# Three edits to a hybrid GLA/FoX/memory layer: an earlier accumulating load for the gates' seventh product, the first gate's T1 built by loads, and mask adds held behind a split

## The chip, the cores and the metric

The kernel runs on one core of one Trainium2 chip. The metric is the device time of one execution in microseconds; lower is better. The engines are named as in the profile: PE (TensorE, matmuls and turns), PEld (its weight loads), DVE (VectorE), ACT (ScalarE), POOL (GpSimd) and SP (SyncE, which here only issues loads). A DMA is issued by a queue of SP, ACT or POOL.

## The reference

One layer on 512 frames of width 1024, all in float32. Three branches read the same normed input `u`; each ends in a projection to width 1024, is weighted by a sigmoid gate, and the sum goes through one more projection.

```python
u = rmsnorm(h, g_mix[l])
proj = u @ w_in[l]
(gq, gk, gv, gg, ga, fq, fk, fv, ff, mq, gates) = split_cols(proj, PROJ_SIZES)
...                                  # branch A: chunked gated linear attention (GLA)
o_fox = forgetting_attention(...)    # branch B: softmax(q k^T * scale + F_t - F_s, causal) v, 8 heads
...                                  # branch C: cross attention into 256 memory tokens
gt = jax.nn.sigmoid(gates.reshape(B, S, N_BRANCH, D))
merged = gt[:, :, 0] * y_gla + gt[:, :, 1] * y_fox + gt[:, :, 2] * y_mem
h = h + merged @ w_out[l]
u2 = rmsnorm(h, g_ffn[l])
h = h + jnp.square(jax.nn.relu(u2 @ w_ff1[l])) @ w_ff2[l]
return rmsnorm(h, g_final)
```

## The kernel before

**Number format.** Every float32 matmul is made of three: each operand is split into a high part (a cast by ACT to the matmul's rounded float32, `hi`) and a low part (the rest, a subtraction by DVE, `lo`), and `mm3` (L163 to L166) issues hi x hi, hi x lo and lo x hi. So each 512 KB tile of weights (128 x 1024) costs one load, one ACT cast and one DVE subtraction, and PE follows them.

**Stages.** In order: memory keys and values, FoX projections and attention, memory attention, GLA, the three gates, output projection, MLP in four quarters. PE's order is written out by hand. The order of the other engines is set by a scheduler that simulates times, except inside `in_order(...)` (L131), where DVE, ACT and SP, and POOL too if it is named, keep the order of the program text. `tc.issue_after(x)` puts an instruction behind `x`.

**FoX.** Heads go in pairs `j`. For each head, `fox_rows` loads a row of decays, spread over all partitions, into `nFb` (L631, issued by ACT). `fox_masks` (L638) adds the causal mask to it in place: two DVE adds a head (L643). `fox_scores` (L645) uses `nFb` in the pair's scores (L670). `fox_turn` (L677) turns one head's probabilities on PE in three banks and splits each into `PTh` (ACT, L217) and `PTl` (DVE, L218); `fox_values` (L691) multiplies them with the values (L697, L698) and sums two halves into `oT` (L706). The list `steps` (L746 to L751) sets the sequence: scores of pair j, rows of pair j+1, values, turn of the even head, its values, masks of pair j+1, turn of the odd head. Projections and GLA weights are woven in between as filling for PE. In `live` lie things that one step leaves for another; `low_parts` (L619) issues put-off low parts behind a given instruction.

**Gates.** Each gate is a matrix product of `u` (512 x 1024) with a 1024 x 1024 weight, done in 2 x 2 blocks by Strassen's scheme in Winograd's form: seven products of blocks (256 x 512 times 512 x 512) instead of eight, in the order `ORDER = (1, 2, 5, 3, 6, 7, 4)`. There are three gates g = 0 (FoX), 1 (memory), 2 (GLA). A round (g, n) is one product: 2 row blocks t of 12 matmuls each, 24 in all. The weights of products 1, 2 and 3 are the blocks "11", "21" and "22" themselves. Products 5, 6, 4 and 7 need sums of blocks, two 512 KB tiles (c = 0, 1) each:

```python
# sum_tile(g, c, 0): "11" -> +"12" (T1, product 5) -> +"22" (product 6) -> +"21" (product 4)
# sum_tile(g, c, 1): "12" -> +"22" (product 7)
```

`load_sum` (L1073) loads the first block on SP's queue. `plus` (L1076) adds another with an accumulating DMA on POOL's queue (L1077). In `low` (L1092) the next `plus` on `sum_tile(g, c, 0)` follows the low part of products 1, 5 and 6. For the first gate, T1 is made another way: `gate_ready` (L988) loads and splits the blocks "11" for product 1 ahead of the gates, inside GLA, and keeps the raw tiles; `first_sum` (L1191) adds "12" to them on DVE after product 1's first half. Until then the tiles of T1 hold the weights of product 2.

Within a round the text's order is: `loads`; matmuls of t = 0; up to two merges of finished gate parts (for g = 1 also an add on POOL, L1171); casts and low parts of the next round's weights (`high`, `low`); `after`; matmuls of t = 1; evacuations of t = 0 and t = 1 (`evac`, L1129), copies on ACT (L1138, L1145, L1150), adds on DVE (L1053), and a tanh on ACT (L1125). Products 1, 6, 7 and 4 share a pair of banks, so product 4 must wait for the evacuation of product 7. `plus(g, c, 1, "22")` stands in `after` of round (g, 5).

Raw tiles that are not sums come from a ring of three (tag `raw`); the tiles of the sums (`h_tile`, tags h0 to h3) lie where GLA's inputs were and can be loaded once those have been read.

## Time and profile before

| | us |
|---|---|
| Median of 3 runs | 818.01 (817.62 to 818.79) |
| The profiled execution | 818.88 |
| Its span in the profile | 817.1 |
| PE busy | 798.7 (98%) |
| DVE busy | 606.6 (74%) |
| ACT busy | 459.3 (56%) |
| POOL busy | 104.9 (13%) |

All times in what follows are microseconds from the start of the span. In a row of a timeline, the bracket says how long the engine had been idle before and what ended that; `x2` means that two instructions are merged into one row. A profile's line number (L1094) is a line of the kernel; helpers such as `vec` (L1053) and `mm3` stand for many places. A releaser is inferred: where it had long been done, it was another, often a DMA.

### The profile page before, as it was taken

The page shows a single profiled execution, that of the slowest core. Times are in us where ns is not written, and L with a number is a line of the kernel's source. Part 1 is how long each engine was busy: PE and PEld are TensorE (multiplying, and loading weights), DVE is VectorE, ACT ScalarE, POOL GpSimd, SP SyncE. Part 2 cuts the span into 40 slices and gives each one's busy share as a digit, 9 for nine tenths or more (in the row PEclk, how much of TensorE's full clock was granted, in tenths as well). Part 3 has the DMA queues.
Part 4 walks back from the last instruction along what each step waited for, and adds up shares of the span by engine and source line. Part 5 has one row for each costly group of instructions (what it writes and reads, how often), then busy time and mean ns, then how long its engine had stood idle before and what let it go on. Part 6 is the DMA issues. An engine that isn't in the chain of part 4 may idle for free.

```text
span 817.1 us, 11695 instructions
## 1 busy us (share of the span) xinstructions
PE 798.7 (98%) x4375; PEld 681.3 (83%) x4375; DVE 606.6 (74%) x945; ACT 459.3 (56%) x733; POOL 104.9 (13%) x135
## 2 busy tenths in 40 slices
PE   9999999999999999998999999999999999999996
PEld 7888877888888877776888889987998899889985
DVE  6878788465545788768565568879799779988896
ACT  7756665444543445544442447775667367647764
POOL 0001000220210112146210000011001100110011
PEclk9999999999999999998999999999999999999998
DMA  9344654999994229796969723898858865895643
GB/s 354 137 168 168 223 208 163 267 248 277 299 325 162 93 105 221 220 178 175 219 149 251 263 79 115 273 234 214 248 180 183 219 217 181 188 274 201 162 84 123
DMA packets 40489, 164.39 MB, mean 201 GB/s; under 512 B 4848, under 2 KB 5552, under 8 KB 38064
## 3 DMA queue, kind: packets, MB, share of 16 engines
q0 software_dynamic: 10784, 61.87, 34.9%
q1 hardware_dynamic: 28288, 97.81, 33.3%
q10 hardware_dynamic: 1360, 3.96, 1.3%
q8 instruction: 34, 0.56, 0.3%
q14 instruction: 23, 0.19, 0.1%
HBM read 161.50 MB, written 35.68 MB: 241 GB/s over the span
## 4 chain that ended last, share of the span: by engine, by line
PE 75%; DMA 9%; DVE 6%; issue 5%; ACT 3%; POOL 1%; POOLq 0%; DVEq 0%; ACTq 0%
PE mm L1325 14%; PE mm L164 12%; PE mm L165 12%; PE mm L166 12%; PE a L164 4%; PE a L166 4%; PE a L165 4%; DMA wb<-in_wst_dram 4%; PE mm L1654 3%; DMA raw<-in_wst_dram 3%; PE mm L385 1%; DMA b<-in_wst_dram 1%; PE mm L1655 1%; PE a L398 1%; DVE wlo L155 1%
## 5 line engine op out<-in xcount | busy, mean ns | idle before, releaser
L1384 ACT CAST hi<-raw 128x1024 fp32r<-128x1024 f32 x52 | 54.5, 1048 | 37.4 <-PE mm L1325 19.2
L1385 DVE TENSOR_TENSOR lo<-raw,hi 128x1024 fp32r<-128x1024 f32 x52 | 63.6, 1223 | 13.5 <-ACT hi L1384 13.3
L155 DVE TENSOR_TENSOR wlo<-raw,whi 128x1024 fp32r<-128x1024 f32 x38 | 46.5, 1222 | 34.9 <-ACT whi L154 34.9
L1325 PE MATMUL mm<-u,hi 128*128 128x256 f32 x384 | 65.1, 283 | 0.0
L154 ACT CAST whi<-raw 128x1024 fp32r<-128x1024 f32 x38 | 39.9, 1050 | 44.2 <-PE mm L165 14.3
L1704 POOL DMA_DIRECT2D b<-in_wst_dram x30 | 25.7, 857 | 263.4 <-DVE lo L1385 130.4
L164 PE MATMUL mm<-uhl,whi 128*128 128x512 f32 x144 | 57.6, 400 | 0.0
L1325 PEld LDWEIGHTS mm<-u,hi 128*128 128x128 f32 x384 | 56.8, 191 | 0.3
L166 PE MATMUL mm<-uhl,wlo 128*128 128x512 f32 x144 | 56.3, 391 | 0.0
L165 PE MATMUL mm<-uhl,whi 128*128 128x512 f32 x144 | 56.2, 390 | 0.0
L165 PE MATMUL mm<-lo,ch 128*128 128x512 f32 (+1 forms) x132 | 51.2, 388 | 0.3 <-DVE lo L1385 0.3
L164 PE MATMUL mm<-hi,ch 128*128 128x512 f32 (+1 forms) x132 | 50.9, 386 | 0.0
L166 PE MATMUL mm<-hi,cl 128*128 128x512 f32 (+1 forms) x132 | 50.9, 386 | 0.0
L1325 PE MATMUL mm<-u2s,hi 128*128 128x256 f32 x288 | 47.6, 283 | 0.0
L1325 PE MATMUL mm<-u,lo 128*128 128x256 f32 x192 | 47.5, 283 | 0.0
L1384 ACT CAST hi<-b 128x1024 fp32r<-128x1024 f32 x26 | 27.3, 1048 | 29.3 <-PE mm L166 19.1
L1094 DVE TENSOR_TENSOR lo<-wb,hi 128x1024 fp32r<-128x1024 f32 x22 | 29.6, 1370 | 17.4 <-ACT hi L1090 17.4
L1325 PEld LDWEIGHTS mm<-u2s,hi 128*128 128x128 f32 x288 | 41.8, 192 | 0.3
L1385 DVE TENSOR_TENSOR lo<-b,hi 128x1024 fp32r<-128x1024 f32 x26 | 31.7, 1221 | 10.8 <-ACT hi L1384 10.8
L165 PE MATMUL a<-lo,ch 128*128 128x512 f32 (+1 forms) x96 | 37.1, 386 | 0.4 <-DVE lo L1442 0.4
L164 PE MATMUL a<-hi,ch 128*128 128x512 f32 (+1 forms) x96 | 37.0, 385 | 0.0
L166 PE MATMUL a<-hi,cl 128*128 128x512 f32 (+1 forms) x96 | 37.0, 385 | 0.0
(508 smaller groups left out, 2316.6 us busy)
## 6 DMA issues: line engine op xcount, KB each, us to landing
raw<-in_wst_dram SPq DMA_DIRECT2D x108, 512.0 KB
raw<-T SPq DMA_DIRECT2D x32, 512.0 KB
b<-in_wst_dram POOLq DMA_DIRECT2D x32, 512.0 KB, 5.2
T<-in_wst_dram POOLq DMA_DIRECT2D x12, 1024.0 KB, 18.2
wb<-in_wst_dram POOLq DMA_DIRECT2D x22, 512.0 KB, 8.0
b<-in_wst_dram SPq DMA_DIRECT2D x16, 512.0 KB
T<-in_wst_dram POOLq DMA_DIRECT2D x12, 512.0 KB, 7.4
wb<-in_wst_dram SPq DMA_DIRECT2D x12, 512.0 KB
```

Of the source, the lines that this page charges most:

```text
L154: cast = nc.scalar.copy(hi, raw)
L155: low_now[0] = nc.vector.tensor_tensor(lo, raw, f(hi), op=ALU.subtract).ins
L164: nc.tensor.matmul(ps, lh, rh, start=start, stop=False, skip_group_check=on)
L165: nc.tensor.matmul(ps, lh, rl, start=False, stop=False, skip_group_check=on)
L166: nc.tensor.matmul(ps, ll, rh, start=False, stop=stop, skip_group_check=on)
L385: nc.tensor.matmul(kps[h], w[:, h * P:(h + 1) * P], x[:, k, :], start=k == p == 0, stop=k == KT - 1 and p == 2)
L1094: nc.vector.tensor_tensor(lo, source(r, c), f(hi), op=ALU.subtract)
L1325: nc.tensor.matmul(ps[:, a, :], x[:, a, k, :], y[:, s, k, :], start=start, stop=stop, skip_group_check=go is not None)
L1384: split_now[0] = nc.scalar.copy(hi, raw).ins
L1385: split_now[1] = nc.vector.tensor_tensor(lo, raw, f(hi), op=ALU.subtract).ins
L1654: nc.tensor.matmul(ps, wh[:, a, k, :], u[:, :, k, :], start=k == 0, stop=False, skip_group_check=True)
L1704: nc.gpsimd.dma_start(to[i], wst[index["B", q, i, x]], accum_op=ALU.add)
```

## The change

Three edits:

1. `fox_turn` keeps the low-part split of its third bank in `live["turn"]`, and for pairs j > 0 the mask adds are issued behind it. By the list of steps that is the turn of the even head of the pair before.
2. The first gate's T1 is made as for the other gates: "11" is loaded into `sum_tile(0, n, 0)` and "12" into `sum_tile(0, n, 1)` on SP, and "12" is accumulated into the first on POOL, all ahead of round (0, 1). `first_sum` is gone, `gate_ready` no longer keeps its raw tiles, and the weights of product 2 go to the ring of raw tiles; the loads of product 3's two tiles stand one round earlier in the text.
3. `plus(g, c, 1, "22")` moves from `after` to `loads` of round (g, 5), for all three gates: ahead of the round's merges and of the casts for product 3.

```diff
@@ fox_masks
-                    nc.vector.tensor_tensor(nFb[:, b, :], nFb[:, b, :], m, op=ALU.add)
+                    with tc.issue_after(live["turn"]) if j else ExitStack():
+                        nc.vector.tensor_tensor(nFb[:, b, :], nFb[:, b, :], m, op=ALU.add)
@@ fox_turn
-            low_parts(split(PTh[:, 1152:1408], PTl[:, 1152:1408], b2[:, :256]))
+            live["turn"] = split(PTh[:, 1152:1408], PTl[:, 1152:1408], b2[:, :256])
+            low_parts(live["turn"])
@@ gate_ready
-            raw = load_w(gate_key("gate_fox", 1, n))
-            ready.append((raw, split_w(raw)))
+            ready.append(get_w(gate_key("gate_fox", 1, n)))
@@
-        def first_sum(n):
-            vec(sum_tile(0, n, 0), ready[n][0], sum_tile(0, n, 1))
@@
         for g in range(3):
             for c in range(2):
-                if g:
-                    at(loads, (g, 1), get, (g, 2), c, shift=-3)
+                at(loads, (g, 1), get, (g, 2), c, shift=-3)
             for c in range(2):
-                at(loads, (g, 1), get, (g, 3), c, shift=c if g else 1)
-                at(after, (g, 5), plus, g, c, 1, "22")
+                at(loads, (g, 1), get, (g, 3), c, shift=c)
+                at(loads, (g, 5), plus, g, c, 1, "22")
...
-        for r, fn, *args in (((0, 1), first_sum, 0), ((0, 1), first_sum, 1), ((0, 5), left, S2, xsum[2]), ((0, 5), sum_three),
+        for r, fn, *args in (((0, 5), left, S2, xsum[2]), ((0, 5), sum_three),
...
-        ws.update({((0, 1), n): w for n, (_, w) in enumerate(ready)})
+        ws.update({((0, 1), n): w for n, w in enumerate(ready)})
...
         with in_order(mybir.EngineType.Pool):
+            for other in range(2):
+                for n in range(2):
+                    load_sum(0, n, other)
             for n in range(2):
-                load_sum(0, n, 1)
-            for n in range(2):
-                raws[(0, 2), n] = sum_tile(0, n, 0)
-                nc.sync.dma_start(raws[(0, 2), n], wst[index[gate_key("gate_fox", 2, n)]])
+                plus(0, n, 0, "12")
```

## The prediction

> **What bounds the kernel now.** The page's first part comes first: the end is set by TensorE.

> ```profile
> PE 798.7 (98%) x4375; PEld 681.3 (83%) x4375; DVE 606.6 (74%) x945; ACT 459.3 (56%) x733; POOL 104.9 (13%) x135
> ```

> Of a span of 817.1 us PE is idle 18.4, much of it at the two ends, and the change touches no matmul. So I went next through PE's own timeline and kept the rows with an idle time in brackets that the change could reach, in the FoX attention and in the gates. The columns are start, duration, engine, line, operation.

> ```profile
> 107.57 0.50 PE L698 MATMUL a<-PTl,V 128*128 128x512 f32 x1 [1.02 <-DVE PTl L218]
> 127.93 0.50 PE L698 MATMUL a<-PTl,V 128*128 128x512 f32 x1 [0.42 <-DVE PTl L218]
> 313.20 0.50 PE L164 MATMUL mm<-hi,s 128*128 128x512 f32 x1 [0.38 <-ACT ct L1145]
> 324.81 0.50 PE L164 MATMUL mm<-hi,uhl 128*128 128x512 f32 x1 [0.39 <-ACT ct L1150]
> 332.17 0.47 PE L164 MATMUL mm<-hi,uhl 128*128 128x512 f32 x1 [1.63 <-DVE ct L1053]
> 375.67 0.77 PE L164 MATMUL mm<-hi,uhl 128*128 128x512 f32 x1 [3.79 <-DVE ct L1053]
> ```

> Two stand at FoX products 2 and 4 (the values of heads 2 and 4), four in the gates: ahead of the first gate's products 3, 7 and 4 and of the second gate's product 4. This last costs more than its 3.79: the matmuls behind it run slow. The table by stretches, and the matmuls that end the slow part:

> ```profile
> 375.00:380.00 5.00, 4.33 (x10) 3.47 (x11) 3.88 (x5) 2.94 (x3) 1.98 (x2) 0.50 0.65 238
> 381.88 0.39 PE L164 MATMUL mm<-hi,uhl 128*128 128x512 f32 x1
> 389.13 0.39 PE L166 MATMUL mm<-hi,uhl 128*128 128x512 f32 x1
> ```

> The granted clock (third number from the end) is 0.50. From 375.67 to 381.88 PE issues 15 matmuls, 6.21 us; from 381.88 to 389.13 it issues 32, 0.227 each, so 15 should take 3.40. The lost clock costs 2.8 us.

> **Part 1, the masks.** What PE waits for at 107.57 is the low half of the turned probabilities (PTl), and VectorE's timeline says why that is late:

> ```profile
> 102.78 0.76 DVE L643 TENSOR_TENSOR nFb<-nFb,cst_s 128x128 f32<-128x128 f32 x2 [2.51 <-DMA nFb<-dF]
> 106.83 1.29 DVE L218 TENSOR_TENSOR PTl<-a,PTh 128x512 fp32r<-128x512 f32 x2
> ```

> DVE works in order and stands 2.51 us before a mask add whose rows have not landed; the head's output sum (oT), two other low parts and PTl are queued behind it. The change puts these adds (four per pair of heads, two times 0.76) behind PTl of the even head. Then DVE goes on at 100.3 (102.78 less 2.51), and PTl comes up to 2.5 + 1.5 us earlier, before 105; PE wants it at 106.4. The adds then run behind it, and their reader, the next pair's scores, comes only after the odd head's turn (PE at 108.96, below), so their own 1.5 us are hidden by the 2.5 us of idle time that they leave; without that cover they would cost 1.5 us for each of three pairs. Nothing else waits for them. The cost of the stall is read from the whole product, not from the bracket alone, since its later matmuls also trickle:

> ```profile
> 106.17 0.39 PE L697 MATMUL a<-PTh,V 128*128 128x512 f32 x1
> 108.96 0.60 PE L681 MATMUL a<-cst_s,Pt 128*128 128x128 f32 x4
> 117.90 0.39 PE L697 MATMUL a<-PTh,V 128*128 128x512 f32 x1
> 119.18 0.40 PE L164 MATMUL mm<-uhl,whi 128*128 128x512 f32 x1
> 127.13 0.39 PE L697 MATMUL a<-PTh,V 128*128 128x512 f32 x1
> 129.32 0.60 PE L681 MATMUL a<-cst_s,Pt 128*128 128x128 f32 x4
> ```

> Start to next step: 2.79 us, an undisturbed one 1.28 (117.90 to 119.18), and 2.19. So 1.51 + 0.91 = 2.4 us to gain; bounds 0 (the adds come late anyhow) and 2.4. I take 2.4, because DVE has 2.5 us to give back against the 1.4 it was late. The masks of pair 1 already had their rows and stop nothing: 0.

> **Part 2, the first gate's T1.** T1 = block 11 + block 12 was two VectorE adds; it becomes two more loads on SP's queue and two accumulating loads on POOL's. The weights of product 2 go to the ring of raw tiles instead of T1's tiles.

> ```profile
> 302.84 2.36 DVE L1053 TENSOR_TENSOR wb<-raw,wb 128x1024 f32<-128x1024 f32 x2
> 306.71 0.94 POOL L1077 DMA_DIRECT2D wb<-in_wst_dram  x1 [14.24 <-DVE lo L1094]
> 307.85 2.64 POOL L1077 DMA_DIRECT2D wb<-in_wst_dram  x3 [0.20 <-issue]
> 320.76 1.05 ACT L1090 CAST hi<-wb 128x1024 fp32r<-128x1024 f32 x1 [1.88 <-DMA wb<-in_wst_dram]
> 323.22 1.05 ACT L1090 CAST f0h<-wb 128x1024 fp32r<-128x1024 f32 x1 [1.42 <-DMA wb<-in_wst_dram]
> 324.18 1.07 ACT L1150 COPY ct<-mm 128x512 f32<-128x512 f32 x2
> 326.77 1.06 ACT L1125 ACTIVATE ct<-ct 128x1024 f32<-128x1024 f32 x1 [1.52 <-DVE ct L1053]
> 290.00:300.00 10.00, 10.00 (x49) 8.15 (x48) 7.35 (x16) 3.07 (x6) 1.91 (x1) 1.00 0.03 11
> ```

> The adds hold VectorE 2.36 us just ahead of product 5's low parts; POOL waits for these before it issues four accumulating loads, two for product 6 and, behind them, the two for product 7. Product 7's land at 320.7 and 323.2, and ACT waits for both. Without the adds POOL starts about 1.7 us sooner (the cast of product 5 must still follow the evacuation of product 1), so product 7's tiles land near 319 and 321.4. The evacuation of product 6 (324.18, two copies in a row, held back by the late cast) then follows PE: the first copy is done in time, the second starts when PE ends, and only 0.55 us of copy and 0.65 of add (the bracket of 1.52 at the tanh, which covers both adds, says so much) stand before the tanh: 325.4 instead of 326.77, 1.4 us sooner. Behind the tanh in ACT's and DVE's order come product 4's casts and low parts and the evacuation for which PE waits at 332.17. The 0.38 at 313.20 goes too (product 2's evacuation starts earlier); it is inside the 1.4. Bounds: 0, and the three gaps together, 0.38 + 0.39 + 1.63 = 2.4. I take 1.4; what is late next is the chain PE, copy, add, tanh, two casts, low part, add, which is longer than one product of 24 matmuls (24 x 0.227 = 5.4 us). The four added DMAs I cost at nothing: in the ten microseconds before the gate the DMA engines are 0.03 busy, and product 2's weights keep their place on SP behind the first gate's other loads, well ahead of their cast (both rows stand at rival d). SP's later loads (product 3's, then the second gate's) wait, as now, for the low part of the third raw tile before them; what is queued behind a late one is weights that are cast later still.

> **Part 3, the seventh sum issued earlier.** In the first gate POOL has nothing between, so the place changes nothing. In the second it moves past POOL's two merge adds:

> ```profile
> 347.55 0.87 POOL L1077 DMA_DIRECT2D wb<-in_wst_dram  x1 [0.27 <-DVE f0l L1094]
> 351.37 3.91 POOL L1171 TENSOR_TENSOR acc<-acc,ct 128x512 f32<-128x512 f32 x2 [2.95 <-DVE ct L1170]
> 355.23 1.76 POOL L1077 DMA_DIRECT2D wb<-in_wst_dram  x2
> 364.56 1.05 ACT L1090 CAST hi<-wb 128x1024 fp32r<-128x1024 f32 x1 [2.68 <-PE mm L165]
> 365.66 0.39 PE L166 MATMUL mm<-f0h,f1l 128*128 128x512 f32 x1
> 366.15 0.50 PE L164 MATMUL mm<-hi,uhl 128*128 128x512 f32 x1
> 365.52 1.15 ACT L1150 COPY ct<-mm 128x512 f32<-128x512 f32 x2
> 368.10 1.06 ACT L1125 ACTIVATE ct<-ct 128x1024 f32<-128x1024 f32 x1 [1.43 <-DVE ct L1053]
> 370.41 2.31 DVE L1094 TENSOR_TENSOR lo<-wb,hi 128x1024 fp32r<-128x1024 f32 x1
> ```

> It is issued at 348.4 instead of 355.23, 6.8 us earlier; POOL is done with it at 350.2, before its adds can start, so nobody behind it waits. The second cast of product 7 (364.56; PE is named its releaser, but the chain of waits has the landing of this tile there) moves forward by some 4 us. But that is worth little: the second copy of product 6 is bound to PE's end of that product (365.66 + 0.39), so copy 0.57 and add 0.65 bring the tanh to 367.4 instead of 368.10, 0.7 us sooner. Behind it stand two merges and two low parts of 2.31 us each (1.2 elsewhere; POOL's adds run beside them), as before. PE's start at 375.67 moves 0.7. Bounds 0 and 3.79; I take 0.7. The gap itself shrinks to 3.79 - 0.7 + 0.25 = 3.3 us, since product 7, which now starts 0.49 behind the matmul before it instead of 0.23, loses that wait. The third gate has neither merges nor PE gaps: 0.

> **The clock.** The 2.8 us stay in my sum: the drop came with a gap of 3.79, the 1.63 at 332.17 brought none, and 3.3 is nearer to the first; bounds 0 and 2.8 gained. [...]

> **Sum.** 2.4 + 1.4 + 0.7 = 4.5 us. The profiled execution took 818.88 in all (span 817.1 and 1.8 around it) and becomes 814.4; it is 0.9 above the median of the three runs, 818.01, which becomes 813.5.

> **Rivals.** (a) The gap ahead of the second gate's product 4 gets short enough that the clock holds: 813.5 - 2.8 = 810.7. For it speaks that 1.63 did not drop it. (b) The sums do not come sooner, because the accumulating loads are bound by their queue and not by their issue (product 7's two are taken 2.5 us apart, at 320.76 and 323.22): only part 1 counts, 815.6. (c) The 2.4 us of part 1 are absorbed before the gates, where ACT waits for a weight:

> ```profile
> 250.71 1.04 ACT L154 CAST whi<-raw 128x1024 fp32r<-128x1024 f32 x1 [4.52 <-DMA raw<-in_wst_dram]
> ```

> Then 815.9. Against it: the loads there are issued behind low parts and casts that PE paces, so they move along. (d) Slower: POOL's queue. If T1's accumulating loads stand ahead of GLA's power on POOL and their tiles are loaded late, that power waits.

> ```profile
> 259.99 0.68 DVE L908 TENSOR_TENSOR qneg<-gqT,ex 128x512 f32<-128x512 f32 x1
> 283.15 0.90 SPq L1245 DMA_DIRECT2D wb<-in_wst_dram  x2
> 287.32 1.91 POOL L972 TENSOR_TENSOR stat<-stat,mhalf 128x4 f32<-128x4 f32 x1 [14.89 <-DVE stat L971]
> 299.49 1.04 ACT L1090 CAST hi<-wb 128x1024 fp32r<-128x1024 f32 x1
> ```

> Loads asked for at 283 land near 290, two issues of 0.9 follow, and the power starts at 292 instead of 287.3: 4.5 us on the chain that ends in the cast at 299.49, which PE's product 2 takes at once, so 4.5 of PE idle and 2.8 of clock against 4.5 gained: 820.8. It decides from a power later than 289 on. Against it: T1's tiles lie over the GLA's decays, keys and queries, last read at 260.7, so their loads need not wait until 283.

> **How the numbers follow.** Forecast 0.52, (a) 0.18, (b) 0.11, (c) 0.06, (d) 0.06, and 0.07 that nothing moves by more than 0.2% (1.6 us, about what can be told from no change here). Faster: 0.52 + 0.18 + 0.11 + 0.06 = 0.87; same 0.07; slower 0.06. The range reaches from under (a) to over (b) and (c), 809.9 to 816.2, and leaves out (d) and no change.

> **What would show it.** Right: no idle before FoX products 2 and 4, mask rows behind PTl; the first gate's tanh of product 6 about 1.4 us nearer to PE's end of that product; the second gate's accumulate right behind the one for product 6, and a gap of 3.3 ahead of its product 4 with a half clock behind it. Wrong: a POOL power that waits, a clock that stays at 1.00, or gaps as long as now.

## The result and the profile after

The changed kernel takes 815.0 us (median; 812.09 to 818.01) where the kernel before, run beside it, takes 818.72 (816.24 to 823.07). The ratio, taken over all runs and not from the two medians, is 0.9949, with an interval of 0.9933 to 0.9964: 0.4 to 0.7% faster, 4.2 us by the ratio and 3.7 by the medians. The forecast of 813.5 was a ratio of 0.9945 to the median of three runs shown (818.01); over more runs that median is 0.7 higher, which is half of the miss of 1.5 us. The profiled execution of the changed kernel took 815.12, span 813.3, against 818.88 and 817.1.

The first part of the page after, then PE's timeline with the rows that carry an idle time (gates and GLA; the last row is the last matmul):

```profile
PE 795.4 (98%) x4375; PEld 680.9 (84%) x4375; DVE 604.8 (74%) x943; ACT 459.1 (56%) x733; POOL 105.6 (13%) x137
```

```profile
253.47 1.97 PE L891 MATMUL a<-cst_s,la 128*128 128x128 f32 x8 [2.15 <-DVE at L952]
...
331.91 0.47 PE L164 MATMUL mm<-hi,uhl 128*128 128x512 f32 x1 [1.36 <-DVE ct L1054]
356.16 0.50 PE L165 MATMUL mm<-lo,s 128*128 128x512 f32 x1 [0.59 <-DVE lo L1095]
374.70 0.47 PE L164 MATMUL mm<-hi,uhl 128*128 128x512 f32 x1 [3.52 <-DVE ct L1054]
386.91 0.50 PE L165 MATMUL a<-lo,uhl 128*128 128x512 f32 x1 [0.41 <-DVE lo L1095]
...
805.41 0.28 PE L166 MATMUL mm<-hi,cl 128*128 128x256 f32 x1
```

The idle rows at FoX products 2 and 4 and at the first gate's products 3 and 7 are gone. The 1.63 ahead of its product 4 is 1.36, the 3.79 in the second gate is 3.52. A new one of 2.15 stands at 253, in the GLA, where the kernel before has 0.23.

VectorE in the FoX attention shows why the first two went: the low half (PTl, 106.83 before) runs at 104.16, and the four mask adds stand behind it in one row without a wait.

```profile
104.16 1.29 DVE L218 TENSOR_TENSOR PTl<-a,PTh 128x512 fp32r<-128x512 f32 x2
106.89 1.42 DVE L644 TENSOR_TENSOR nFb<-nFb,cst_s 128x128 f32<-128x128 f32 x4
```

To see where a gain goes I took the same instruction in both traces and subtracted the starts. Here are rows of ScalarE, first of the kernel before and then of the one after:

```profile
232.91 1.05 ACT L154 CAST whi<-raw 128x1024 fp32r<-128x1024 f32 x1 [0.77 <-PE mm L166]
278.02 0.62 ACT L217 CAST og<-og 128x512 fp32r<-128x512 f32 x1 [2.62 <-DVE og L983]
```

```profile
230.75 1.05 ACT L154 CAST whi<-raw 128x1024 fp32r<-128x1024 f32 x1 [0.77 <-PE mm L166]
250.48 1.05 ACT L154 CAST whi<-raw 128x1024 fp32r<-128x1024 f32 x1 [6.44 <-DMA raw<-in_wst_dram]
279.40 0.62 ACT L217 CAST og<-og 128x512 fp32r<-128x512 f32 x1 [2.62 <-DVE og L985]
367.12 1.06 ACT L1126 ACTIVATE ct<-ct 128x1024 f32<-128x1024 f32 x1 [0.76 <-DVE ct L1054]
406.93 1.05 ACT L1091 CAST f0h<-wb 128x1024 fp32r<-128x1024 f32 x1 [2.81 <-DMA wb<-in_wst_dram]
```

After minus before is -2.16 at 231; -0.23 at the cast of 250.48, which waits 6.44 for its weight; +1.38 at 279; -0.26 at the first gate's product 4 (331.91 against 332.17); -0.97 at the second gate's (374.70 against 375.67); and -3.93 at the last matmul, which stands at 809.34 before:

```profile
809.34 0.28 PE L166 MATMUL mm<-hi,cl 128*128 128x256 f32 x1
```

Two of these steps are the clock, as the table by stretches after says (granted clock third from the end):

```profile
253.47:257.00 3.53, 3.53 (x13) 3.14 (x14) 3.36 (x10) 0.60 (x1) 0.00 (x0) 0.52 0.43 154
375.00:380.00 5.00, 5.00 (x23) 4.13 (x22) 3.87 (x5) 3.44 (x4) 2.95 (x2) 1.00 0.55 205
```

The 2.15 at 253 is followed by a half clock, so that stage loses 1.9 us of idle time and some 1.6 of clock. The 3.52 at 374.70 is not followed by one: the matmuls behind it gain 2.7 us by 382. But 1.1 of that is given back by 390, where the third gate's first product waits for a low part (the row of 386.91), which the kernel before does not. The last 1.5 us come in the MLP, between 549 and 565, where the kernel before waits (0.42 at 549.50, 0.32 at 558.31) in code that the change does not touch. So this execution gained 2.2 up to 231 us, lost 3.5 in the GLA, gained 1.6 in the first gate, 0.7 in the second, 1.6 net by the clock and 1.5 in the MLP, less some 0.2 in between.

POOL's timeline shows the moved loads. GLA's powers (L974) go ahead of T1's accumulating loads; the first gate's sums are issued from 306.32 on; and in the second gate the seventh sums stand in one row with the sixth, ahead of the adds:

```profile
288.71 1.91 POOL L974 TENSOR_TENSOR stat<-stat,mhalf 128x4 f32<-128x4 f32 x1 [14.91 <-DVE stat L973]
...
293.81 1.84 POOL L1078 DMA_DIRECT2D wb<-in_wst_dram  x2
306.32 0.85 POOL L1078 DMA_DIRECT2D wb<-in_wst_dram  x1 [10.68 <-DVE lo L1095]
...
347.30 2.65 POOL L1078 DMA_DIRECT2D wb<-in_wst_dram  x3 [0.28 <-DVE f0l L1095]
351.11 3.90 POOL L1172 TENSOR_TENSOR acc<-acc,ct 128x512 f32<-128x512 f32 x2 [1.17 <-DVE ct L1171]
```

### The profile page after: what moved, and what is told of

The parts are those of the page before. It is cut to its first block, busy times and chain, and to the rows that moved or that the text cites. A ratio compares the mean times of both kernels' runs of the same rounds, so it can differ in the third digit from the quotient of the medians.

```text
span 813.3 us, 11700 instructions
## 1 busy us (share of the span) xinstructions
PE 795.4 (98%) x4375; PEld 680.9 (84%) x4375; DVE 604.8 (74%) x943; ACT 459.1 (56%) x733; POOL 105.6 (13%) x137
## 4 chain that ended last, share of the span: by engine, by line
PE 84%; DVE 5%; DMA 5%; issue 3%; ACT 2%; POOL 1%; POOLq 0%; DVEq 0%; ACTq 0%
PE mm L1322 16%; PE mm L164 14%; PE mm L165 13%; PE mm L166 13%; PE a L165 5%; PE a L166 5%; PE a L164 5%; PE mm L1651 3%; DMA wb<-in_wst_dram 3%; DMA raw<-in_wst_dram 2%; PE mm L385 1%; PE mm L1652 1%; DVE lo L1095 1%; PE a L398 1%; DVE wlo L155 1%
## 5 line engine op out<-in xcount | busy, mean ns | idle before, releaser
L154 ACT CAST whi<-raw 128x1024 fp32r<-128x1024 f32 x38 | 39.9, 1050 | 47.5 <-PE mm L165 15.0
L164 PE MATMUL mm<-uhl,whi 128*128 128x512 f32 x144 | 57.6, 400 | 0.0
L166 PE MATMUL mm<-uhl,wlo 128*128 128x512 f32 x144 | 56.3, 391 | 0.0
L165 PE MATMUL mm<-uhl,whi 128*128 128x512 f32 x144 | 56.1, 390 | 0.0
L164 PE MATMUL mm<-hi,ch 128*128 128x512 f32 (+1 forms) x132 | 50.9, 386 | 0.0
L165 PE MATMUL mm<-lo,ch 128*128 128x512 f32 (+1 forms) x132 | 50.9, 386 | 0.0
L166 PE MATMUL mm<-hi,cl 128*128 128x512 f32 (+1 forms) x132 | 50.9, 386 | 0.0
L165 PE MATMUL a<-lo,ch 128*128 128x512 f32 (+1 forms) x96 | 37.0, 385 | 0.0
L164 PE MATMUL a<-hi,ch 128*128 128x512 f32 (+1 forms) x96 | 37.0, 385 | 0.0
L166 PE MATMUL a<-hi,cl 128*128 128x512 f32 (+1 forms) x96 | 36.9, 385 | 0.0
```

The source lines that it names most:

```text
L154: cast = nc.scalar.copy(hi, raw)
L164: nc.tensor.matmul(ps, lh, rh, start=start, stop=False, skip_group_check=on)
L165: nc.tensor.matmul(ps, lh, rl, start=False, stop=False, skip_group_check=on)
L166: nc.tensor.matmul(ps, ll, rh, start=False, stop=stop, skip_group_check=on)
```

## The experiments

**Each part alone.** Three kernels, each the kernel before with one part of the change: the masks (the first two hunks), T1 by loads (`first_sum` out, `plus(0, n, 0, "12")` and the two further loads in), and the seventh sum:

```diff
-                at(after, (g, 5), plus, g, c, 1, "22")
+                at(loads, (g, 5), plus, g, c, 1, "22")
```

Masks alone, expected:

> Only the mask adds are held back; gates as before. Theory A (PE gains 2.4 us in FoX, and all PE-paced work moves that much earlier, but one weight load that lands near 250 us is bound by the DMA engines and does not): no idle before FoX products 2 and 4, the cast of the weight near 250.5 as before, an idle time of about 2.1 us ahead of the matmul at 253.5 where there was 0.23, gates as before; gain 2.4 - 1.9 = 0.5 us, ratio 0.998 to 1.001. Rival B (the stall at 253 comes from the new loads of T1, not from the shift): no idle there, ratio 0.997.

T1 alone, expected:

> Only T1 by accumulating loads; the seventh sum still issued in the second half of the round, masks as before. Theory A: idle at 253 stays at 0.2; the gaps ahead of the first gate's products 3 and 7 (0.38, 0.39) go, the one ahead of product 4 falls from 1.63 to 1.4: 1.0 to 1.6 us gained, ratio 0.998; the second gate's gap of 3.8 stays. Rival B: an idle time of 2 us at 253, ratio 1.000.

Seventh sum alone, expected:

> Only the accumulate for product 7 issued earlier. Theory A: the first gate is unchanged; in the second the cast of product 7's second tile moves 4 us forward, the tanh of product 6 only 0.7, the gap ahead of product 4 from 3.8 to 3.5: 0.7 us gained, ratio 0.999, and up to 2.8 more in executions where the clock holds. Rival C (the tanh is bound by the tiles' landing, not by PE's end of product 6): 2 us or more, gap under 2.

Measured against 818.21 of the kernel before: masks 816.39, ratio 0.9972 (0.9952 to 0.9991); T1 816.37, 0.9981 (0.9961 to 1.0002); seventh sum 817.74, 0.9991 (0.9965 to 1.0017). In us by the ratios: 2.3, 1.6 and 0.7, each with some 1.6 to 2 either way, so that only the masks are told from nothing; the sum is 4.6, the whole change 4.2. A row of each: ScalarE's with the masks alone, then PE's with T1 alone and with the seventh sum alone:

```profile
246.97 1.04 ACT L154 CAST whi<-raw 128x1024 fp32r<-128x1024 f32 x1 [2.93 <-DMA raw<-in_wst_dram]
```

```profile
331.31 0.47 PE L164 MATMUL mm<-hi,uhl 128*128 128x512 f32 x1 [1.35 <-DVE ct L1052]
```

```profile
259.37 1.85 PE L889 MATMUL a<-cst_s,la 128*128 128x128 f32 x7 [2.06 <-DVE at L950]
```

With the masks alone the late weight of 250.48 is cast at 246.97 and PE does not wait in the GLA. With the seventh sum alone, which touches nothing ahead of the gates, PE waits 2.06 there (in an execution of 824.55 us, the slowest of its twelve). So the wait at 253 does not come from the masks' new place; it comes and goes with the execution. Theory A of the masks, which had a wait of 2.1 there, was wrong, and so was its rival's reason, T1's new loads: T1 alone waits 0.54. The rival's ratio of 0.997 is the one that came. With T1 alone the small gaps of the first gate go and 1.35 is left ahead of product 4, as in the whole change.

The thirteen profiles of this document (the other kernels follow below) say more of the parts than the medians do, when the same matmuls are compared with those of the kernel before. The FoX attention (104 to 135 us) is 2.41 us shorter in each of the eight kernels with the masks' new place. In the four others with the old place it is between 1.01 shorter and 3.23 longer, and VectorE waits 1.80 to 3.70 us for the mask rows in them and in the kernel before. From 290 us to the first gate's product 4, the seven kernels with T1 by loads and the old order of merges gain 1.53 to 1.68; the three others without T1 by loads lie between a loss of 0.02 and a gain of 0.57. The seventh sum is another matter. Where it is issued early, with the old order of merges, the second gate gains 0.68 to 0.72 up to its product 4. But it gains 0.72 and 0.66 in the kernels with the masks alone and with T1 alone, which issue it as late as before:

```profile
371.77 0.77 PE L164 MATMUL mm<-hi,uhl 128*128 128x512 f32 x1 [3.51 <-DVE ct L1055]
374.18 0.76 PE L164 MATMUL mm<-hi,uhl 128*128 128x512 f32 x1 [3.57 <-DVE ct L1052]
```

The gap was 3.79 before; the kernel before with the sooner sums (below) gains 0.18 here. So with the late issue the tile sometimes lands in time and sometimes does not, and the 0.7 is not shown to be the earlier issue's own.

**The late weight.** Up to there the DMA engines also carry 35 sums of weights from memory to memory, on POOL's queue. One run holds back two of them until after the gates:

```diff
-    sums = [islice(sum_ops(), *x) for x in ((35,), (35, None))]
+    sums = [islice(sum_ops(), *x) for x in ((33,), (33, None))]
```

> The changed kernel, with the last two of the 35 early DRAM sums for the MLP put off to the output projection. Theory A (the load near 250 is late because the sums' queue fills the DMA engines): the weight's cast moves from 250.5 to below 247, the 2.15 us of idle at 253 fall under 0.4, and 2 us and the half clock behind the stall are gained: ratio to the kernel before 0.991. Rival D (the load is late for another reason, such as its own queue): idle at 253 stays near 2, ratio 0.995.

It took 816.77, 0.9978 (0.9960 to 0.9996), some 2 us more than the whole change, with intervals that just touch; the theory had 0.991. The weight is cast at 244.92 and the wait at 253 is gone, as the theory had it, but new ones stand at 461 to 471, behind the sums that are now issued from 414 on (ScalarE's row, then PE's):

```profile
244.92 1.05 ACT L154 CAST whi<-raw 128x1024 fp32r<-128x1024 f32 x1 [1.41 <-PE mm L165]
```

```profile
461.54 0.50 PE L164 MATMUL a<-hi,mh 128*128 128x512 f32 x1 [0.88 <-ACT mh L1184]
...
471.29 0.50 PE L165 MATMUL mm<-wlo,mh 128*128 128x512 f32 x1 [0.77 <-DVE wlo L155]
```

The sums make the weight late; moved behind the gates they go with other waits. The next run moves four of them the other way, to where the DMA engines have room:

```diff
-        for to, src, add_ in islice(sums[len(late_on)], 1 if late_on or chunk_n[0] <= 14 else 2):
+        for to, src, add_ in islice(sums[len(late_on)], 1 if late_on or chunk_n[0] <= 10 else 2):
```

> The changed kernel, with four of the 35 early weight sums (memory to memory, on POOL's queue) issued sooner: two per weight cast from the 11th cast on instead of the 15th (around 105 us instead of 138). Nothing moves behind the gates, unlike the run with 33 sums. The DMA engines are full from 160 to 245 us (shares 0.91 to 1.16) and half full at 100 to 140 (0.48 to 0.69). Theory (the weight whose cast stands at 250.5 lands late because the sums fill the DMA engines, and that swallows the 2.4 us of the masks): the cast comes 2 us or more sooner, PE does not idle near 253, the clock holds there, and with no new stall at 461 to 472 the time is some 2 to 3.5 below the changed kernel: 811.5 to 813. Rival (that landing is bound by the ring of raw tiles or by SP, or the DMA engines are as full at 100 to 140): no change, or new waits in FoX: 815 to 817.

811.85 (810.9 to 812.96), 0.9927 (0.9903 to 0.9951): 3 us below the whole change by the medians, 1.8 by the ratios, whose intervals overlap. Its 6 runs lie 2 us apart, the 18 of the whole change 6. The stretches (DMA share next to last), of the changed kernel and then with the sooner sums, and in the latter the cast:

```profile
100.00:140.00 40.00, 40.00 (x235) 33.50 (x234) 34.57 (x101) 24.84 (x59) 2.91 (x6) 1.00 0.59 202
160.00:245.00 85.00, 85.00 (x423) 71.90 (x422) 47.19 (x81) 38.88 (x80) 14.55 (x24) 1.00 1.04 288
```

```profile
100.00:140.00 40.00, 40.00 (x235) 33.53 (x234) 33.95 (x99) 25.11 (x60) 5.87 (x10) 1.00 0.81 269
160.00:245.00 85.00, 85.00 (x423) 71.87 (x421) 47.29 (x81) 38.69 (x81) 10.97 (x19) 1.00 0.97 281
```

```profile
244.79 1.05 ACT L154 CAST whi<-raw 128x1024 fp32r<-128x1024 f32 x1 [1.41 <-PE mm L165]
```

The cast now waits for PE and not for its weight. So it is in all six kernels here with fewer or sooner sums: in none of their profiles does PE wait at 253, and from 245 to 290 us each takes 44.51 us. The seven other profiles take between 44.51 (masks alone) and 48.55.

**The change on that ground.** With the sooner sums in both, does the change bring its sum? Two more kernels, parts 2 and 3 without the masks, and the kernel before:

> The four sums issued sooner, with parts 2 and 3 of the change but the FoX masks in their old place. Theory (the masks are worth their 2.4 us wherever no late weight swallows them): 2 to 3 above the kernel with all three parts and the sooner sums (811.85), so 814 to 815. The rows that the masks wait for come by the same DMA engines, which are now fuller at 100 to 140 us (0.81 instead of 0.59), so the difference may be larger. Rival (PE's idle time in FoX is given back before the gates in any case): 812 to 812.5.

> The kernel before with nothing changed but the four sums issued sooner. Theory (before waits little for that weight: 0.23 us of PE at 253.7 in its profile, though more in some executions): 0 to 1.5 below before, with a narrower spread, so some 817 to 818; and the whole change is then worth 5 to 6 (811.85 against it), 4.5 from its three parts and the rest from the wait that they would have run into. Rival (the sooner sums help before as much as they helped the changed kernel, 3 us): 815 to 815.5, and the change is worth 3.5 with or without them.

Without the masks 814.34, 0.9955 (0.9935 to 0.9975); the kernel before 815.72, 0.9960 (0.9944 to 0.9976). By the medians the masks are worth 2.5 us (814.34 to 811.85) and the whole change 3.9; by the ratios 2.3 and 2.7, of which only the second is clear of its noise, some 2.4. My theory that before would gain little from the sooner sums was wrong: it gains 0.4%, as its rival had it. The same cast without the masks, and before with the sooner sums, each in its ScalarE timeline:

```profile
246.38 1.05 ACT L154 CAST whi<-raw 128x1024 fp32r<-128x1024 f32 x1 [1.41 <-PE mm L165]
```

```profile
247.52 1.05 ACT L154 CAST whi<-raw 128x1024 fp32r<-128x1024 f32 x1 [1.41 <-PE mm L165]
```

Against 244.79 that is 1.59 and 2.73 later. These differences arise in FoX and are still the same at 290 us: nothing swallows them once the weight is on time. These two kernels have the same FoX and yet differ by 1.14: the rows that the masks wait for are also transfers that come when they can (VectorE waits 1.80 and 2.58 us for them in the one, 3.05 and 2.57 in the other). That may be why, without the masks' new place, the 12 runs lie 6.3 us apart again.

**The clock.** 12 matmuls whose result nobody reads fill PE's idle time ahead of the second gate's product 4, first on the changed kernel, then with the sooner sums too:

```diff
+                if r == (1, 4):
+                    fill = [at_() for _ in range(2)]
+                    for k in range(12):
+                        nc.tensor.matmul(fill[k % 2], uhi[:, 0, 0:128], ws[(1, 7), 0][0][:, 0:512], start=True, stop=True)
```

> The changed kernel, with 12 matmuls of 128x512 (0.227 us each, 2.7 in all, into banks that nobody reads) ahead of the second gate's product 4, where PE otherwise idles 3.5 us. They end about 0.8 us before product 4 can start, so the work that follows starts no sooner; only PE's idle time is gone. Theory (the median of the changed kernel hides a mixture: in most executions the clock drops behind the 3.5 us gap, at 2.8 us, in some it does not): the median falls by 1.5 to 2.8 to some 813, the half clock behind product 4 is gone from the profile, and the start of product 4 stays. Rival (the clock costs nothing in the end, because what follows waits for something else): the median stays at 815, with the half clock gone.

> The changed kernel with the four sums issued sooner (811.85 by itself, runs from 810.9 to 813.0) and, on top, the 12 matmuls into unread banks ahead of the second gate's product 4. There the half clock stood from 369.84 to 373.25 in the profile, worth 1.6 us. Theory (the lost clock counts, and in the run with fillers alone it was later waits for transfers at 384 to 472 us that took it back): with those waits gone, the fillers now bring 1 to 2 us: 810 to 811. Rival (the clock behind this gap is never paid for, since evacuations and casts set the pace of the gate): 811.5 to 812.5, as without fillers.

815.46, 0.9963 (0.9944 to 0.9982), against 0.9949 without fillers; and 812.73, 0.9929 (0.9903 to 0.9956), against 811.85. The clock held in both profiles (matmuls 0.23 apart behind 372.01 in the first, 1.00 in the stretch of the second below), and neither kernel is faster. The stretch behind product 4 with the sooner sums alone, then with the fillers too:

```profile
370.00:375.00 5.00, 5.00 (x15) 4.00 (x16) 3.88 (x4) 3.33 (x4) 2.68 (x2) 0.67 0.60 210
370.00:375.00 5.00, 4.74 (x21) 3.94 (x22) 3.87 (x5) 3.44 (x4) 2.38 (x2) 1.00 0.57 210
```

PE of the first filler run and its ScalarE, then PE and ScalarE of the second:

```profile
252.28 1.16 PE L891 MATMUL a<-cst_s,la 128*128 128x128 f32 x8 [0.58 <-DVE at L952]
372.01 0.47 PE L164 MATMUL mm<-hi,uhl 128*128 128x512 f32 x1 [0.83 <-DVE ct L1054]
384.22 0.50 PE L165 MATMUL a<-lo,uhl 128*128 128x512 f32 x1 [0.41 <-DVE lo L1095]
407.20 0.50 PE L164 MATMUL mm<-hi,uhl 128*128 128x512 f32 x1 [1.15 <-ACT ct L1151]
```

```profile
405.62 1.05 ACT L1091 CAST f0h<-wb 128x1024 fp32r<-128x1024 f32 x1 [2.76 <-DMA wb<-in_wst_dram]
452.13 1.05 ACT L1091 CAST hi<-raw 128x1024 fp32r<-128x1024 f32 x1 [6.23 <-DMA raw<-in_wst_dram]
```

```profile
370.26 0.47 PE L164 MATMUL mm<-hi,uhl 128*128 128x512 f32 x1 [0.82 <-DVE ct L1054]
```

```profile
450.11 1.05 ACT L1091 CAST hi<-raw 128x1024 fp32r<-128x1024 f32 x1 [6.87 <-DMA raw<-in_wst_dram]
```

The rival holds: what the clock gives is waited out behind it. With the sooner sums, where the run without fillers had the half clock, the fillers bring 1.5 us up to 376. Of these 1.1 are gone by 385, where the third gate's first product waits for a low part, and 0.5 by 410; at 470, in the output projection, the filler run is 2.3 behind, since its weights land later (the cast of 450.11 stands at 447.59 without fillers). In the first filler run, 2.7 us ahead of the changed kernel at 372, 1.4 go by 407 (the cast of 405.62 against 406.93) and the rest by 452 (against 451.91 there). The program up to 370 is the changed kernel's own, instruction for instruction, and its wait at 252 is 0.58 where that one has 2.15: once more, that wait is the execution's. Why the transfers behind the gates keep their hour in one run and move along in another, and whether the fillers have a part in it, stays open.

**The order on VectorE.** The 3.52 that are left in the second gate are a chain of VectorE's: two merges, two low parts of 2.3 beside POOL's adds, the subtraction. A kernel with the merges behind the subtraction of the first tiles:

```diff
                     if t:
                         evac(r, t - 1)
+                    if t == 1:
+                        for x in parts:
+                            merge(*x)
...
                     if t == 0:
-                        for x in parts:
-                            merge(*x)
```

> The changed kernel, with the two merges of a gate's product moved behind the evacuation of its first row of tiles (they stood ahead of the next product's low parts). Nothing is left out. Theory (the gap ahead of the second gate's product 4 is VectorE's order: two merges of 0.64, then two low parts of 2.3 each that run beside POOL's adds, then the subtraction that frees the bank): without merges ahead, the low parts take 1.2 each and start 1.2 sooner, so the gap of 3.52 becomes about 1.2, the small gaps of 0.4 to 0.6 after gate products go, and no clock drops there in any execution. Gain over the changed kernel 2.3, or about 4 where that one loses the clock: 811 to 813. Rival (the adds beside the low parts only move): the merges now set POOL's adds beside the low parts of the NEXT product, PE waits 1 to 1.5 us there, and 814 to 815 remains.

813.14, 0.9945 (0.9926 to 0.9964), not told apart from 0.9949. VectorE, then PE:

```profile
365.92 1.22 DVE L1095 TENSOR_TENSOR lo<-wb,hi 128x1024 fp32r<-128x1024 f32 x1 [2.06 <-ACT hi L1091]
367.83 1.23 DVE L1095 TENSOR_TENSOR f0l<-wb,f0h 128x1024 fp32r<-128x1024 f32 x1 [0.69 <-ACT f0h L1091]
```

```profile
329.58 0.47 PE L164 MATMUL mm<-hi,uhl 128*128 128x512 f32 x1 [1.99 <-DVE ct L1054]
369.80 0.63 PE L164 MATMUL mm<-hi,uhl 128*128 128x512 f32 x1 [1.85 <-DVE ct L1054]
405.20 0.50 PE L164 MATMUL mm<-hi,uhl 128*128 128x512 f32 x1 [0.88 <-ACT ct L1151]
```

The low parts fall from 2.3 to 1.2 and the gap from 3.52 to 1.85 (1.2 was expected; VectorE now waits 0.69 for the second cast), and a half clock still follows it in this profile, which the theory had excluded. Against that the first gate's gap grows from 1.36 to 1.99, and 0.88 appear in the third gate, as the rival had it in part. In the changed kernel the two low parts (369.43, 2.32 and 371.67, 2.28) run beside two adds of POOL's (368.99, 3.88 for both); without adds beside them they take the 1.22 and 1.23 of the rows above. What makes them slower beside the adds is not shown.

The sooner sums and this order together, a version that beats both kernels:

> The merge order and the sooner sums together, on the changed kernel. If the two waits (253 us and 372 us) are separate and both theories hold, the gains add: 2 to 4 from the gate, 2 to 3.5 from the weight, 808.5 to 811, with PE idle less than 1.5 us at each place. If either is only displaced, it equals the better of the two alone.

810.53 (809.83 to 811.47), 0.9908 (0.9886 to 0.9929): 1.3 below the sooner sums alone by the medians, with intervals that overlap. PE's idle rows above 0.5 us in the gates:

```profile
328.97 0.47 PE L164 MATMUL mm<-hi,uhl 128*128 128x512 f32 x1 [2.12 <-DVE ct L1054]
369.17 0.47 PE L164 MATMUL mm<-hi,uhl 128*128 128x512 f32 x1 [1.86 <-DVE ct L1054]
```

## Why the prediction was right, and where it was not

**The sum held.** 4.5 us forecast; 4.2 by the ratio, and 2.7 by the ratios (3.9 by the medians) with the sooner sums in both. Term by term: part 1, forecast 2.4, is 2.41 over the FoX attention in every profile that has it (2.2 at 231, since this execution came to FoX 0.25 late), and 2.3 by the ratios, alone and on the sooner sums. Part 2, forecast 1.4, is 1.64 in the profile (+1.38 at 279, -0.26 at product 4) and 1.6 by the ratio, whose interval reaches past zero. Part 3, forecast 0.7, is 0.71 in the profile, but there its number is right by luck, at least in part: two kernels without it gain 0.72 and 0.66 at the same place. I took the late landing in the one profile before for the rule; it is one case among others, and the earlier issue takes that case away. By the ratio it is 0.7, not told from zero. Set against the mean of the few profiles without the part, at the same place, the three are 3.0, 1.4 and 0.3: the sum of 4.7 is near the forecast, but more of it is the masks' and less the seventh sum's. The steps behind them hold too: against the stage's +1.38, POOL's sums of the first gate come 1.8 sooner (306.32 against 306.71; forecast 1.7), and the second gate's tanh comes 0.98 sooner (367.12 against 368.10), of which 0.26 is from ahead of the gate and 0.72 its own (forecast 0.7). The gap behind it, forecast 3.3, is 3.52.

**The absorption (rival c) was argued away for a wrong reason.** I wrote that the loads ahead of the gates move along, since PE paces what they are issued behind. They are issued sooner, but the DMA engines are full from 160 to 245 us (share 1.04), and the weight lands when they get to it: its cast came 0.23 sooner (250.71 to 250.48) for an issue 2.16 sooner. The ring has three raw tiles, so the load for this cast is issued behind the low part of the cast of 232.91 before, and of 230.75 after:

```profile
235.25 0.33 SPq L147 DMA_DIRECT2D raw<-in_wst_dram  x1
233.09 0.33 SPq L147 DMA_DIRECT2D raw<-in_wst_dram  x1
```

In the profiled execution the wait and the half clock behind it swallowed the 2.2 and 1.4 more. The wait differs from execution to execution: 0.52 to 0.58 of idle time in two other kernels that are the same up to there, 2.06 in one without the masks. It can hit both kernels, which fits that the medians keep the masks' gain and that the sooner sums help both. My bracket of 0.23 in the profile before said only that one execution had just escaped.

**The clock was kept in for a poor reason, and it was worth less than 2.8.** I compared the length of the gaps. It does not tell a gap that costs the clock from one that does not: of nine gaps of 3.5 to 3.8 us at this product, eight brought a half clock, the profiled changed kernel's did not. In the last section's table this one differs in how it lies, with 0.56 of its fullest window idle where the three others of this length have 0.65 to 0.99. That execution thus shows rival (a) by luck, and by the prediction's own signs a clock that stays at 1.00 spoke against it; the clock's 1.6 and the MLP's 1.5 repaid most of the 3.5 lost at 253. And the filler runs say that holding the clock there moves the time by nothing that can be measured (the ratios allow a gain of some 1 us in the first and 3 in the second). What failed is the price: of 2.8 us of slow matmuls 1.6 are left by 390, when the third gate's first product has waited for its low part, and these can be lost to later weights. The sum took no gain from the clock, so the forecast did not suffer.

**Rivals (b) and (d)** did not come: the casts of the first gate's product 7 follow the sooner sums (318.81 and 321.54 against 320.76 and 323.22, in a stage that began 1.38 later), and POOL's power ran at 288.71, ahead of T1's loads: 1.39 later than the 287.32 of before, which is the lateness of the whole stage (+1.38), with a wait of 14.91 where it had 14.89.

## What to carry to other kernels

Read the DMA share of the stretch behind the place where you save: if it is near one (1.04 here), a saved microsecond may only be waited out at the next weight, and moving background transfers to a half-empty stretch (share 0.59; here worth 2 to 3 us) can bring nearly as much as the edit. A bracket that is small in one profile is no proof of slack where a landing decides it (0.23 in the profile before, 2.06 in another execution). Price a lost clock by what waits at the end of that stage, not by the slow matmuls (1.6 us here, not 2.8). Before a gain is put down to an edit, look at the same place in kernels without the edit: a single profile before may show a bad case for the rule.

## What the runs showed of the chip that I had not expected

```
kernel               PE idle           idle share of the fullest window   half clock
sooner sums+order    326.85 to 328.97  0.55                               no
after                371.18 to 374.70  0.56 (the next one 0.48)           no
merge order          367.95 to 369.80  0.54                               yes, 3.41 us
seventh sum alone    257.31 to 259.37  0.60                               yes, 3.41 us
after                251.32 to 253.47  0.63                               yes, 3.41 us
masks alone          368.26 to 371.77  0.65 (the next one 0.38)           yes, 6.83 us
before               371.88 to 375.67  0.81 (the next one 0.30)           yes, 6.83 us
sooner sums          366.46 to 369.98  0.99 (the next one 0.04)           yes, 3.41 us
```

In these rows a half clock follows each window that is idle for 0.60 or more. Around 0.55 no border can be read: 0.55 and 0.56 kept the clock and 0.54 lost it, here and at 109.22 above, where two gaps of 0.69 and 1.13 share a window. The half clock lasted for two windows where the next one too was idle for 0.27 to 0.41, and for one where that was idle for 0.11 or less. The gaps of the kernels left out lie the same way. So the gap of 1.85 us cost the clock, and the one of 3.52 in the changed kernel, which the grid splits into 0.56 and 0.48, did not. By what rule the clock is granted is not shown.
